# Second mixer: TensorE in written order with longer assumed latencies, zero-padded keys and factors, the last up-projection begun early

## The chip, the cores and the metric

The kernel runs on one core of a Trainium2 chip. The metric is the device time of one execution, in microseconds (us). An execution is also recorded by the hardware profiler: the rows of its trace are quoted below. PE is TensorE (matrix products), DVE VectorE, ACT ScalarE, POOL GpSimd, SP the engine that issues most of the DMAs.

## What is computed

256 tokens of width 1024 go through two layers (feed-forward, a mixer, feed-forward: a gated delta rule in the first, windowed attention in the second), a norm, and then a second block. Its mixer, which the change is about, is the sum of two gated branches over one input projection:

```python
proj = h @ w_in[i]
attn = windowed_gqa(q, k, v, sink[i])              # 8 query heads, 2 key heads of 64
rw = rwkv7_time_mix(zr, ...)                       # 8 heads of 64, scanned in both directions
gates = jax.nn.sigmoid(proj[..., O_GATE:].reshape(bsz, s, N_BRANCH, D_MODEL))
merged = gates[..., 0, :] * (attn @ w_up_attn[i]) + gates[..., 1, :] * (rw @ w_up_rwkv[i])
x = x + merged @ w_out[i]
```

`rwkv7_time_mix` makes a decay and a rate for each direction from low-rank factors (`w2`, `a2`, rank 64), normalises the keys, and runs this recurrence over the 256 tokens, forward and backward:

```python
sa = jnp.einsum('dbhij,dbhj->dbhi', state, a_t)
state = state * w_t[..., None, :] + sa[..., :, None] * b_t[..., None, :] + v_t[..., :, None] * k_t[..., None, :]
y = jnp.einsum('dbhij,dbhj->dbhi', state, r_t)
```

followed by a group norm, a bonus term and a gate.

## The kernel before

Weights are read as 128 x 1024 float32 tiles (`raw`), split by ACT and DVE into a high and a low half (`wh`, `wl`, L177 and L178), and each product of two split operands is three matmuls. In the second mixer these dense projections have 256 moving columns (`hT` against `wh`, `wl`).

The recurrence is computed in chunks of 64 tokens. The 512 channels make four channel tiles t = 0 to 3 of two heads each; `rw_chain(t)` is one such tile from its projections to its output: factors and decays (L1042 to L1130, tiles `lw`, `ta`, `cen`, `kd`, `BK`, `AR`), products of the factors (AR,BK), a triangular inverse (forward substitution on DVE, L430 to L443, then small products iY,Lc; iT,iX; iX,iT; iY,M on PE), then a scan of four steps over the chunks in both directions (R, UV, S; products UV,M; R,X; UV,bkt; S,AR), the group norm (L1240 to L1251), and the transposes and the gate into `sT[t]`. A step of the scan goes from PE to ACT (copy R, L1207), PE (R,X), DVE and ACT (copies UV, L1217 and L1218), PE (UV,bkt), DVE (state S, L1229) and PE again (S,AR). `gqa_chain` is the attention: a score product for each of 16 pairs of token half and head (kT,gt), a row maximum and exponential, transposes, products with v (v,sTl).

`weave` (L314) writes the five chains and a stream of projections into one program: each chain yields its PE time and the latency until its next step can run, the chain waits that latency times `slack`, and meanwhile projections are emitted. So the order in the program is a plan. In the kernel before, the order on each engine is then set anew by the scheduler of the tile framework, instruction by instruction, with a priority for the chains.

The stream holds the input projections (`p_rkv`, `p_q`, `p_kv`), the gates (`p_gate`) and the up-projections (`p_up`). The up-projection of the recurrent branch, which needs all four `sT[t]`, stands behind all chains, with the output projection `w_out`. Float32 matmuls are two records each in the trace, those on split operands and transposes one.

Of the kernel before, what the change touches and what calls it, by code (L numbers as in the profile page):

```python
# [9 lines left out]
F32 = mybir.dt.float32  # L10
# [5 lines left out]
P = 128  # L16
# [102 lines left out]
def _program(ctx, tc, a, out, stages):  # L119
# [302 lines left out]
    def tri_inverse(tl, Lc, off, nu, sign, unit, X, ydst=None):  # L422
# [551 lines left out]
    def mixer2_body(tl, hT, rstd, sums, finish_norm):  # L974
# [67 lines left out]
        def rw_chain(t):  # L1042
# [5 lines left out]
            w2a2, w0 = tl([256], "w2a2"), tl([256], "w0")  # L1048
            nc.sync.dma_start(w2a2, a["w2a2"][t])
# [4 lines left out]
            for m in range(2):  # L1054
                mm(ps[:, m * 256:(m + 1) * 256], wa[0:64, m * P:(m + 1) * P], w2a2[0:64])
# [5 lines left out]
            while state["k"][t] is None:  # L1061
                yield 0, 0.5
            k_ = state["k"][t]
# [21 lines left out]
            pbon = bank()  # L1085
            for d in range(2):
                ps = bank()
                mm(ps[:, 0:256], w2a2[64:128, d * P:(d + 1) * P], wa[64:128, :])
# [42 lines left out]
                yield 0.1, 2.0  # L1131
# [110 lines left out]
            for g in range(4):  # L1242
                junk = tl([64], "junk64")
                nc.scalar.activation(junk, py[:, g * 64:(g + 1) * 64], AF.Square, bias=nmean[:, g:g + 1],
                                     accum_out=var[:, g:g + 1])
# [12 lines left out]
            yield 0, 3.5  # L1258
# [32 lines left out]
        def gqa_chain():  # L1291
# [9 lines left out]
            kT, vs, qT = tl([256], "kT"), [], []  # L1301
            for m in range(2):
# [22 lines left out]
                ra, rb_, rc, rd = (tl([10, 8], f"rot{j}") for j in range(4))  # L1325
# [6 lines left out]
                yield 0, 6.0  # L1332
# [8 lines left out]
                nc.scalar.copy(kT[:, m * P:(m + 1) * P], ps[:, 0:P])  # L1341
# [4 lines left out]
            def scores(m, t, e):  # L1346
                hd, r = e * 4 + t, slice(e * 64, e * 64 + 64)
# [3 lines left out]
                ps = bank()  # L1351
                mm(ps[:, 0:256], qT[m][r, t * P:(t + 1) * P], kT[r, :])
                sm, mx = tl([256], "sTh", 4), tl([1], "mx", 2)
                nc.vector.tensor_tensor_reduce(out=sm, in0=ps[:, 0:256], in1=C(f"near{m}"), scale=1.0, scalar=-3e38,
                                               op0=ALU.add, op1=ALU.max, accum_out=mx)
                nc.vector.tensor_scalar(nm[:, hd:hd + 1], mx, -0.125, nsk[:, hd:hd + 1], ALU.mult, ALU.min)
                nc.scalar.activation(sm, sm, AF.Exp, scale=0.125, bias=nm[:, hd:hd + 1], accum_out=den[:, hd:hd + 1])
                return m, hd, e, sm
# [27 lines left out]
            todo = [(m, t, e) for m in range(2) for t in range(4) for e in range(2)]  # L1386
# [18 lines left out]
        def block_steps(src, blocks, ps):  # L1405
            for i, ap in enumerate(blocks):
                w = weights(ap)
                for q in range(4):
                    k = 4 * i + q
                    for h in range(2):  # L1410
                        for j, (l, r) in enumerate(((0, 0), (0, 1), (1, 0))):
                            mm(ps[:, h * 256:(h + 1) * 256], src[k][l][:, h * P:(h + 1) * P], w[r][:, q * 256:(q + 1) * 256],
                               k == 0 and h == 0 and j == 0, k == len(src) - 1 and j == 2, skip_group_check=True)
# [16 lines left out]

        def p_up(br, nb, pool=psA):
            ps = bank(pool)
            src = sTa if br == 0 else [sT[t] for t in range(NT)]
            yield from block_steps(src, [a["w_up_rwkv" if br else "w_up_attn"][nb]], ps)
# [30 lines left out]

        def stream():
# [8 lines left out]
        weave([rw_chain(t) for t in range(NT)] + [gqa_chain()], stream(), share=0.25, ahead=150, slack=0.95)  # L1475
# [220 lines left out]
```

## Time and profile before

| what | value |
| --- | --- |
| three timed runs, median | 1610.34 us (1604.14 to 1625.45) |
| the profiled execution's own time | 1610.71 us |
| its span in the trace | 1608.9 us |
| granted TensorE clock, mean over the span | 0.971 of full speed |
| PE busy | 1573.1 us, 98% of the span, 10608 records |
| DVE, ACT busy | 1097.5 us (68%), 919.4 us (57%) |

Busy times add up what an engine's records cover; on PE the ends of matmuls are modelled, so a high share does not mean that each matmul takes its shortest time. The interval from one start to the next is the better measure of a matmul's cost, and is used below.

### The profile page before, as it was taken

The page shows a single profiled execution, that of the slowest core. Times are in us where ns is not written, and L with a number is a line of the kernel's source. Part 1 is how long each engine was busy: PE and PEld are TensorE (multiplying, and loading weights), DVE is VectorE, ACT ScalarE, POOL GpSimd, SP SyncE. Part 2 cuts the span into 40 slices and gives each one's busy share as a digit, 9 for nine tenths or more (in the row PEclk, how much of TensorE's full clock was granted, in tenths as well). Part 3 has the DMA queues.
Part 4 walks back from the last instruction along what each step waited for, and adds up shares of the span by engine and source line. Part 5 has one row for each costly group of instructions (what it writes and reads, how often), then busy time and mean ns, then how long its engine had stood idle before and what let it go on. Part 6 is the DMA issues. An engine that isn't in the chain of part 4 may idle for free.

```text
span 1608.9 us, 28081 instructions
## 1 busy us (share of the span) xinstructions
PE 1573.1 (98%) x10608; PEld 1331.6 (83%) x10608; DVE 1097.5 (68%) x2691; ACT 919.4 (57%) x1998; POOL 36.6 (2%) x47
## 2 busy tenths in 40 slices
PE   7999998999999999999999999999999999999998
PEld 6888887997888888888888888888777788778887
DVE  6666779677766767666767766777756455776665
ACT  7555576666655555555546555575554444665553
POOL 0000010010000000000100000000000000000000
PEclk9999999999999999999999999998979679999999
DMA  7666523344766646665325766543211123565551
GB/s 230 208 197 196 172 61 107 100 150 133 236 195 197 192 135 212 197 198 161 118 90 161 212 196 199 165 143 112 70 31 32 36 83 119 177 223 194 195 185 55
DMA packets 71128, 244.18 MB, mean 152 GB/s; under 512 B 8400, under 2 KB 12240, under 8 KB 70992
## 3 DMA queue, kind: packets, MB, share of 16 engines
q1 hardware_dynamic: 70992, 242.39, 48.6%
q8 instruction: 83, 1.36, 0.3%
q14 instruction: 53, 0.43, 0.1%
HBM read 241.31 MB, written 1.05 MB: 151 GB/s over the span
## 4 chain that ended last, share of the span: by engine, by line
PE 76%; DVE 10%; DMA 8%; ACT 3%; issue 2%; POOL 1%; SPq 0%; ACTq 0%; DVEq 0%; POOLq 0%
PE bank L189 17%; PE bank L197 17%; PE bank L182 10%; PE bank L184 10%; PE bank L183 10%; PE bank L190 9%; DMA raw<-in_ffn_w_dram 5%; DVE wl L178 5%; ACT wh L177 2%; DMA raw<-in_w_ff_dram 1%; DVE cacc L596 1%; PE bank L248 1%; POOL rn L200 0%; DVE gs L194 0%; PE bank L1363 0%
## 5 line engine op out<-in xcount | busy, mean ns | idle before, releaser
L178 DVE TENSOR_TENSOR wl<-raw,wh 128x512 fp32r<-128x512 f32 (+1 forms) x714 | 574.8, 827 | 218.7 <-ACT wh L177 212.7
L177 ACT CAST wh<-raw 128x512 fp32r<-128x512 f32 (+1 forms) x714 | 497.4, 731 | 298.5 <-DMA raw<-in_ffn_w_dram 170.3
L189 PE MATMUL bank<-hT,wh 128*128 128x512 f32 x1664 | 587.6, 396 | 3.6 <-DVE hT L255 3.5
L190 PE MATMUL bank<-hT,wl 128*128 128x256 f32 x1664 | 463.3, 279 | 0.2 <-DVE wl L178 0.2
L189 PEld LDWEIGHTS bank<-hT,wh 128*128 128x128 f32 x1664 | 312.7, 188 | 77.6 <-DVE hT L255 5.7
L190 PEld LDWEIGHTS bank<-hT,wl 128*128 128x128 f32 x1664 | 313.5, 188 | 5.0 <-DVE wl L178 0.7
L182 PE MATMUL bank<-wh,aT 128*128 128x512 f32 x584 | 232.2, 398 | 3.1 <-ACT aT L216 2.8
L184 PE MATMUL bank<-wh,aT 128*128 128x512 f32 x584 | 229.1, 395 | 1.0 <-DVE aT L217 1.0
L183 PE MATMUL bank<-wl,aT 128*128 128x512 f32 x584 | 228.4, 391 | 0.0
L182 PEld LDWEIGHTS bank<-wh,aT 128*128 128x128 f32 x584 | 109.6, 188 | 29.0 <-ACT aT L216 5.4
L184 PEld LDWEIGHTS bank<-wh,aT 128*128 128x128 f32 x584 | 109.5, 188 | 28.9 <-DVE aT L217 3.6
L183 PEld LDWEIGHTS bank<-wl,aT 128*128 128x128 f32 x584 | 109.8, 188 | 19.7
L182 PE MATMUL bank<-hT,wh 128*128 128x256 f32 x384 | 114.3, 298 | 1.7 <-ACT wh L177 1.7
L184 PE MATMUL bank<-hT,wl 128*128 128x256 f32 x384 | 112.5, 294 | 0.6 <-DVE wl L178 0.6
L183 PE MATMUL bank<-hT,wh 128*128 128x256 f32 x384 | 112.7, 294 | 0.0
L402 ACT ACTIVATE gs<-gs 128x256 f32<-128x256 f32 x88 | 36.8, 418 | 85.9 <-DVE gs L401 85.9
L194 DVE TENSOR_TENSOR av<-av,bank 128x256 f32<-128x256 f32 x120 | 50.0, 418 | 43.9 <-ACT av L193 43.2
L182 PEld LDWEIGHTS bank<-hT,wh 128*128 128x128 f32 x384 | 75.6, 197 | 4.3 <-ACT wh L177 1.9
L184 PEld LDWEIGHTS bank<-hT,wl 128*128 128x128 f32 x384 | 75.4, 197 | 3.5 <-issue 2.1
L183 PEld LDWEIGHTS bank<-hT,wh 128*128 128x128 f32 x384 | 75.6, 197 | 2.2 <-issue 1.6
L197 PE MATMUL bank<-wh,hT 128*128 128x256 f32 x256 | 60.8, 322 | 0.1
L216 ACT CAST aT<-av 128x256 fp32r<-128x256 f32 x120 | 48.6, 406 | 21.2 <-DVE av L1519 12.3
(412 smaller groups left out, 2044.9 us busy)
## 6 DMA issues: line engine op xcount, KB each, us to landing
raw<-in_ffn_w_dram SPq DMA_DIRECT2D x264, 512.0 KB, 4.1
raw<-in_w_ff_dram SPq DMA_DIRECT2D x64, 512.0 KB, 4.2
raw<-in_a_w_qkv_dram SPq DMA_DIRECT2D x24, 512.0 KB, 3.7
raw<-in_w_gate_dram SPq DMA_DIRECT2D x16, 512.0 KB, 3.5
raw<-in_w_rwkv_dram SPq DMA_DIRECT2D x14, 512.0 KB, 3.6
raw<-in_b_w_qk_dram SPq DMA_DIRECT2D x10, 512.0 KB, 4.3
raw<-in_a_w_z_dram SPq DMA_DIRECT2D x8, 512.0 KB, 3.6
raw<-in_a_w_out_dram SPq DMA_DIRECT2D x8, 512.0 KB, 3.5
```

What stands on the lines that cost most here:

```text
L177: nc.scalar.copy(hi[:, c], raw[:, c])
L178: nc.vector.tensor_tensor(lo[:, c], raw[:, c], hi.bitcast(F32)[:, c], ALU.subtract)
L182: nc.tensor.matmul(o, l[0], r[0], start=start, stop=False, **kw)
L183: nc.tensor.matmul(o, l[0], r[1], start=False, stop=False, **kw)
L184: nc.tensor.matmul(o, l[1], r[0], start=False, stop=stop, **kw)
L189: nc.tensor.matmul(o, l[0], both, start=start, stop=False, skip_group_check=True)
L190: nc.tensor.matmul(o[:, 0:256], l[1], both[:, 0:256], start=False, stop=stop, skip_group_check=True)
L194: nc.vector.tensor_tensor(t, t, o[:, 0:256], ALU.add)
L197: nc.tensor.matmul(o, lhsT, rhs, start=start, stop=stop, **kw)
L216: nc.scalar.copy(hi, src)
L248: nc.tensor.transpose(ps[:, q * 256 + h * P:q * 256 + (h + 1) * P], x[h][n][:, c * P:(c + 1) * P], ident)
L402: nc.scalar.activation(gs, gs, AF.Silu)
```

## The change

- The second mixer's `weave` runs with the scheduler's reordering switched off for PE alone: PE gets its instructions in the order in which they are written. The other engines are scheduled as before.
- `slack` goes from 0.95 to 1.3, and some yields have longer latencies: 5.0 and 4.0 at the start of chain 0, 7.0 before the bonus products, 11.0 for 6.0 in the attention's prelude, 5.0 for 3.5 before the chain's last transposes.
- The factors of both directions are computed first, the bonus products (kd,rks) come later, with their own bank allocated later.
- The low-rank factors are held in two tiles padded with zeros to 128 rows (`w2z`, `a2z`), so these products have 128 rows; two DMAs for one in each chain.
- The keys are held as two copies padded with zeros (`kT`, [2, 256]): the scores of two heads are one product of 128 rows and 512 columns, 8 in all for 16; the attention goes on in pairs of heads.
- The recurrent branch's up-projection is begun for three of its four column blocks with channel tiles 0 to 2 (`p_begin`), while the last chain runs; `p_up` adds tile 3.
- Some small tiles share buffers with others, and `irow` has two buffers for three (in the first layer's mixer too).

```diff
-                row = tl([nu, 16], "irow", 3)[:, :, 0:k]
+                row = tl([nu, 16], "irow", 2)[:, :, 0:k]
...
+        w2z, a2z = tl([256], "w2z"), tl([256], "a2z")
+        nc.gpsimd.memset(w2z[64:128], 0.0)
+        nc.gpsimd.memset(a2z[0:64], 0.0)
...
-            w2a2, w0 = tl([256], "w2a2"), tl([256], "w0")
-            nc.sync.dma_start(w2a2, a["w2a2"][t])
+            if t == 0:
+                yield 0, 5.0
+            w0 = tl([256], "w0")
+            nc.sync.dma_start(w2z[0:64], a["w2a2"][t][0:64])
+            nc.sync.dma_start(a2z[64:128], a["w2a2"][t][64:128])
...
-                mm(ps[:, m * 256:(m + 1) * 256], wa[0:64, m * P:(m + 1) * P], w2a2[0:64])
+                mm(ps[:, m * 256:(m + 1) * 256], wa[:, m * P:(m + 1) * P], w2z)
...
-                mm(ps[:, 0:256], w2a2[64:128, d * P:(d + 1) * P], wa[64:128, :])
+                mm(ps[:, 0:256], a2z[:, d * P:(d + 1) * P], wa)
...
-                yield 1.3, 2.0
-                while state["r"][t] is None:
-                    yield 0, 0.5
-                r_ = state["r"][t]
+                facs.append((ta, Em, cen, off))
+                yield 0.9, 0
+            while state["r"][t] is None:
+                yield 0, 0.5
+            r_ = state["r"][t]
+            kds = []
+            for d, (ta, Em, cen, off) in enumerate(facs):
...
+                kds.append(kd)
+            yield 0, 7.0
+            pbon = bank()
+            for d, kd in enumerate(kds):
                 for m in range(2):
                     mm(pbon[:, 2 * m:2 * m + 2], kd[:, m * P:(m + 1) * P], rks[:, d * 4 + t], d == 0 and m == 0, d == 1,
...
-            yield 0, 3.5
+            yield 0, 5.0
...
-            kT, vs, qT = tl([256], "kT"), [], []
+            kT, vs, qT = tl([2, 256], "kT"), [], []
+            for e in range(2):
+                nc.gpsimd.memset(kT[64 - e * 64:128 - e * 64, e], 0.0)
...
-                yield 0, 6.0
+                yield 0, 11.0
...
-                mm(ps[:, 0:256], qT[m][r, t * P:(t + 1) * P], kT[r, :])
+                mm(ps, qT[m][:, t * P:(t + 1) * P], flat(kT))
...
-                if q2:
-                    values(*q2.pop(0))
-                if q1:
-                    q2.append(turn(*q1.pop(0)))
-                if todo:
-                    q1.append(scores(*todo.pop(0)))
-                yield 0.9, 1.2
+                for args in q2:
+                    values(*args)
+                q2 = [turn(*args) for args in q1]
+                q1 = scores(*todo.pop(0)) if todo else []
+                yield 1.8, 3.6
...
+        def p_begin(nb):
+            ps, w = begun[nb] = bank(psA), weights(a["w_up_rwkv"][nb])
+            yield from block_steps(sT, [None], ps, w, range(NT - 1))
...
         def p_up(br, nb, pool=psA):
+            if (br, nb) in ((1, k) for k in begun):
+                ps, w = begun[nb]
+                yield from block_steps(sT, [None], ps, w, [NT - 1])
+            else:
...
+        tasks += [(lambda nb=nb: len(gts) == 8 and state["rw"][2] > 2 and (nb < 1 or state["rw"][3] > 1), lambda nb=nb: p_begin(nb))
+                  for nb in range(3)]
...
-        weave([rw_chain(t) for t in range(NT)] + [gqa_chain()], stream(), share=0.25, ahead=150, slack=0.95)
+        with tc.manual_schedule(engines={mybir.EngineType.PE}):
+            weave([rw_chain(t) for t in range(NT)] + [gqa_chain()], stream(), share=0.25, ahead=150, slack=1.3)
```

Three places show what that makes of PE's order. The numbers in the names count the program's tiles, so they differ between the two programs. The first place is the start of the third chain's inverse (products iY,Lc), with a step of another chain's scan (UV,M and S,AR). Before:

```order
L197 MATMUL bank_13925<-iY_13673,Lc_13598 32x32 x6
L197 MATMUL bank_13999<-UV_13995,M_12453 64x64
L197 MATMUL bank_13925<-iY_13673,Lc_13598 32x32
L197 MATMUL bank_13999<-UV_13996,M_12531 64x64
L197 MATMUL bank_13925<-iY_13673,Lc_13598 32x32
L197 MATMUL bank_13999<-UV_13995,M_12453 64x64
L197 MATMUL bank_13925<-iY_13673,Lc_13598 32x32
L197 MATMUL bank_13999<-UV_13996,M_12531 64x64
L197 MATMUL bank_13925<-iY_13673,Lc_13598 32x32
L197 MATMUL bank_13999<-S_13325,AR_12157 64x128
L197 MATMUL bank_13925<-iY_13673,Lc_13598 32x32
```

After, the same chain's inverse, with an up-projection of the attention branch (wh, wl against sTh, sTl) around it:

```order
L197 MATMUL bank_14112<-wh_14115,sTl_13907 128x256
L197 MATMUL bank_14145<-iY_13881,Lc_13806 32x32 x32
L197 MATMUL bank_14112<-wh_14115,sTh_13913 128x256
L197 MATMUL bank_14112<-wl_14116,sTh_13913 128x256
L197 MATMUL bank_14112<-wh_14115,sTl_13914 128x256
L197 MATMUL bank_14112<-wh_14115,sTh_13913 128x256
L197 MATMUL bank_14112<-wl_14116,sTh_13913 128x256
L197 MATMUL bank_14112<-wh_14115,sTl_13914 128x256
L197 MATMUL bank_13669<-UV_14040,M_12882 64x64
L197 MATMUL bank_13669<-UV_14041,M_12947 64x64
L197 MATMUL bank_13669<-UV_14040,M_12882 64x64
L197 MATMUL bank_13669<-UV_14041,M_12947 64x64
```

The inverse's 32 products now stand together, as do the scan's.

The second place is the fourth chain's last step of the scan. Before, with a gate projection (wh, wl against hT) between:

```order
L197 MATMUL bank_15234<-UV_15230,M_14298 64x64
L197 MATMUL bank_14919<-wh_14922,hT_11329 128x256
L197 MATMUL bank_15234<-UV_15231,M_14350 64x64
L197 MATMUL bank_14919<-wl_14923,hT_11329 128x256
L197 MATMUL bank_14919<-wh_14922,hT_11329 128x256 x2
L197 MATMUL bank_15234<-S_14989,AR_14100 64x128 x2
L197 MATMUL bank_14919<-wl_14923,hT_11329 128x256
L197 MATMUL bank_14987<-S_14989,AR_14100 64x128
L197 MATMUL bank_14919<-wh_14922,hT_11329 128x256
L197 MATMUL bank_14987<-S_14989,AR_14100 64x128
L197 MATMUL bank_15247<-R_15241,X641_11372 64x64
```

After:

```order
L197 MATMUL bank_15255<-UV_15251,M_14436 64x64
L197 MATMUL bank_15255<-UV_15252,M_14494 64x64
L197 MATMUL bank_15255<-UV_15251,M_14436 64x64
L197 MATMUL bank_15255<-UV_15252,M_14494 64x64
L197 MATMUL bank_15255<-S_15039,AR_14126 64x128 x2
L197 MATMUL bank_15037<-S_15039,AR_14126 64x128 x2
L197 MATMUL bank_15266<-R_15262,X641_11372 64x64 x4
L197 MATMUL bank_15037<-UV_15251,M_14436 64x64
```

No projection is left between the products of this step, and none between it and the step ahead of it.

The third place is the end of the fourth chain, where its normed output is transposed (`aTl`, `aTh` against the identity in `c_base`) and gated (`gl` with `g2`). Before, among the gate projections:

```order
L197 MATMUL bank_15025<-wh_15084,hT_11429 128x256
L1262 MATMUL bank_15295<-c_base_78,aTh_15286 128x128
L197 MATMUL bank_15025<-wh_15084,hT_11429 128x256
L197 MATMUL bank_15025<-wl_15085,hT_11429 128x256
L197 MATMUL bank_15025<-wh_15084,hT_11429 128x256
L197 MATMUL bank_15025<-wh_15084,hT_11432 128x256
L1262 MATMUL bank_15295<-c_base_78,aTh_15286 128x128
```

After, behind the begun up-projection (tiles of `sT` of the third chain, sTh_15069 and sTl_15070), and ahead of what needs this chain's own output (sTh_15375):

```order
L197 MATMUL bank_15339<-wh_15342,sTh_15069 128x256
L197 MATMUL bank_15339<-wl_15343,sTh_15069 128x256
L197 MATMUL bank_15339<-wh_15342,sTl_15070 128x256
L1278 MATMUL bank_15364<-c_base_78,aTl_15306 128x128 x2
L1278 MATMUL bank_15364<-c_base_78,aTh_15305 128x128 x2
L197 MATMUL bank_15365<-gl_12163,g2_15312 128x256
L197 MATMUL bank_15171<-wh_15174,sTh_15375 128x256
```

All gates have moved ahead of this place; between the transposes and the products that need their result one other matmul stands.

## Rows read from the trace of the kernel before

**Rows 1.** The page, parts 1 and 4: busy time, its share of the span, instructions of each engine; and the chain that ended last, share of the span by engine.

```profile
PE 1573.1 (98%) x10608; PEld 1331.6 (83%) x10608; DVE 1097.5 (68%) x2691; ACT 919.4 (57%) x1998; POOL 36.6 (2%) x47
...
PE 76%; DVE 10%; DMA 8%; ACT 3%; issue 2%; POOL 1%; SPq 0%; ACTq 0%; DVEq 0%; POOLq 0%
```

**Rows 2.** Busy time of each engine in a stretch, the whole region of the second mixer's chains. Columns: stretch in us, its length, then busy us and records of each engine, mean granted clock of TensorE (1 is full), DMA share, GB/s.

```profile
1055.57:1363.58 308.01, 305.04 (x3008) 247.49 (x3009) 193.03 (x724) 160.07 (x400) 0.62 (x2) 0.87 0.23 73
```

**Rows 3.** The largest of PE's waits in that region: line waited at, engine and line waited for; us in total, times, longest.

```profile
PE bank L1363 <- ACT sTh L1357: 1.2, 1, 1.2
```

**Rows 4.** The six stretches of that region in which the granted clock is at half; columns as in the second group. The first of them, and the sum of all.

```profile
1115.00:1125.20 10.20, 10.20 (x70) 7.83 (x70) 4.03 (x12) 4.20 (x10) 0.00 (x0) 0.50 0.30 103
...
sum 81.70, PE 81.70 PEld 61.39 DVE 30.17 ACT 30.67 POOL 0.62; mean PE 13.62 PEld 10.23 DVE 5.03 ACT 5.11 POOL 0.10
```

**Rows 5.** The same columns for a stretch ahead of a fall of the clock and for one of dense gate projections.

```profile
1176.40:1183.30 6.90, 6.90 (x93) 5.21 (x91) 2.91 (x9) 4.30 (x12) 0.00 (x0) 0.99 0.28 79
...
1340.40:1347.20 6.80, 6.80 (x58) 6.80 (x58) 3.81 (x17) 4.74 (x14) 0.00 (x0) 1.00 0.27 80
```

**Rows 6.** PE in order of time, third chain's inverse and a scan. Columns: start, time until the last of the group ends (us), engine, line, operation, out<-in, shape, records in the group.

```profile
1232.59 0.31 PE L197 MATMUL bank<-iY,Lc 32*32 32x32 f32 x12
1232.84 0.33 PE L197 MATMUL bank<-UV,M 64*64 64x64 f32 x2
1233.09 0.24 PE L197 MATMUL bank<-iY,Lc 32*32 32x32 f32 x2
1233.27 0.33 PE L197 MATMUL bank<-UV,M 64*64 64x64 f32 x2
...
1234.38 0.27 PE L197 MATMUL bank<-iY,Lc 32*32 32x32 f32 x2
```

**Rows 7.** PE in order of time, the fourth chain's last two steps of the scan, and the transposes behind its norm; columns as before.

```profile
1326.09 0.66 PE L197 MATMUL bank<-S,AR 128*64 128x128 f32 x8
1326.67 0.39 PE L197 MATMUL bank<-wh,hT 128*128 128x256 f32 x1
...
1327.11 0.45 PE L197 MATMUL bank<-R,X 64*64 64x64 f32 x8
...
1327.85 0.45 PE L197 MATMUL bank<-UV,M 64*64 64x64 f32 x8
1328.23 0.50 PE L197 MATMUL bank<-wh,hT 128*128 128x256 f32 x2
...
1331.64 0.45 PE L197 MATMUL bank<-R,X 64*64 64x64 f32 x8
...
1335.70 0.38 PE L197 MATMUL bank<-wl,hT 128*128 128x256 f32 x1
1336.02 0.43 PE L197 MATMUL bank<-S,AR 128*64 128x128 f32 x2
1336.38 0.39 PE L197 MATMUL bank<-wh,hT 128*128 128x256 f32 x1
...
1347.56 0.33 PE L1262 MATMUL bank<-c_base,aTh 128*128 128x128 f32 x1
```

**Rows 8.** PE in order of time, three places: products of the factors cut off from each other, the same in one block, and a score product; columns as before.

```profile
1079.07 0.71 PE L197 MATMUL bank<-AR,BK 64*128 64x128 f32 x4
1079.71 0.61 PE L197 MATMUL bank<-rks,kd 128*128 128x2 f32 x4
...
1131.64 1.16 PE L197 MATMUL bank<-AR,BK 64*128 64x128 f32 x16
1132.73 0.28 PE L197 MATMUL bank<-zero 128*128 128x256 bf16 x1
...
1178.35 0.70 PE L197 MATMUL bank<-kT,gt 64*128 64x256 f32 x2
1178.98 0.38 PE L197 MATMUL bank<-rks,kd 128*128 128x2 f32 x2
```

**Rows 9.** DVE in order of time, first and last instruction of the third chain's forward substitution.

```profile
1208.99 0.42 DVE L430 TENSOR_TENSOR iLm<-Lc,c_inv 128x256 f32<-128x256 f32 x1
...
1229.66 0.44 DVE L443 STREAM_TRANSPOSE iX<-iY 128x256 f32<-128x256 f32 x1
```

**Rows 10.** DVE's groups of instructions in the region. Columns: line, engine, operation, out<-in, shapes, count, busy us, mean ns of one, idle time before and what ended it.

```profile
L178 DVE TENSOR_TENSOR wl<-raw,wh 128x1024 fp32r<-128x1024 f32 x41 | 49.9, 1220 | 10.7 <-ACT wh L177 10.5
...
L1229 DVE TENSOR_TENSOR S<-bank,sf 64x128 f32<-64x128 f32 x24 | 6.9, 287 | 14.2 <-PE bank L197 13.9
...
L1217 DVE COPY UV<-bank 64x128 f32<-64x128 f32 x16 | 4.6, 288 | 21.3 <-PE bank L197 21.2
```

**Rows 11.** DVE and then ACT in order of time, the tail: norm (L1240 to L1251), gate and split (L1265 to L1275), gated sum (L1436), split for the output projection (L217).

```profile
1340.27 0.42 DVE L1240 TENSOR_REDUCE nmean<-bank 128x4 f32<-128x256 f32 x1 [0.26 <-PE bank L197]
...
1352.06 0.42 DVE L1275 TENSOR_TENSOR sTl<-aTh,sTh 128x256 fp32r<-128x256 f32 x1
...
1357.82 0.68 DVE L1436 SCALAR_TENSOR_TENSOR gt<-gt,bank 128x512 f32<-128x512 f32 x1
...
1361.91 0.76 DVE L217 TENSOR_TENSOR aT<-bank,aT 128x256 fp32r<-128x256 f32 x2
...
1346.81 1.29 ACT L1251 ACTIVATE aTh<-bank,nmean,var 128x64 f32<-128x64 f32 x4
...
1348.52 0.57 ACT L1265 ACTIVATE aTh<-bank,vec 128x256 f32<-128x256 f32 x1 [0.42 <-PE bank L1262]
```

More of the change, by code (lines that the diff above doesn't have):

```diff
@@ L1324, in gqa_chain @@
                 x1, x2 = hx(qk)[:, :, 0:8], hx(qk)[:, :, 8:16]
-                ra, rb_, rc, rd = (tl([10, 8], f"rot{j}") for j in range(4))
+                ra, rb_, rc, rd = (tl([256], "sTl", 4)[:, 0:80].rearrange("p (h s) -> p h s", s=8) for j in range(4))
                 nc.vector.tensor_tensor(ra, x1, cos, ALU.mult)
@@ L1340, in gqa_chain @@
                 nc.tensor.transpose(ps[:, 0:P], qk[:, 512:640], ident)
-                nc.scalar.copy(kT[:, m * P:(m + 1) * P], ps[:, 0:P])
+                for e in range(2):
+                    nc.scalar.copy(kT[e * 64:e * 64 + 64, e, m * P:(m + 1) * P], ps[e * 64:e * 64 + 64, 0:P])
                 yield 0.5, 0.5
@@ L1344, in gqa_chain, with scores @@
             acc = {}
-            def scores(m, t, e):
-                hd, r = e * 4 + t, slice(e * 64, e * 64 + 64)
+            def scores(m, t):
                 if m not in acc:
@@ L1350, in scores @@
                 den, nm = acc[m]
-                ps = bank()
-                mm(ps[:, 0:256], qT[m][r, t * P:(t + 1) * P], kT[r, :])
[L1353 to L1358, printed above, removed]
+                ps, both = bank(), []
+                mm(ps, qT[m][:, t * P:(t + 1) * P], flat(kT))
+                for e in range(2):
+                    hd = e * 4 + t
+                    sm, mx = tl([256], "sTh", 4), tl([1], "mx", 2)
+                    nc.vector.tensor_tensor_reduce(out=sm, in0=ps[:, e * 256:(e + 1) * 256], in1=C(f"near{m}"), scale=1.0,
+                                                   scalar=-3e38, op0=ALU.add, op1=ALU.max, accum_out=mx)
+                    nc.vector.tensor_scalar(nm[:, hd:hd + 1], mx, -0.125, nsk[:, hd:hd + 1], ALU.mult, ALU.min)
+                    nc.scalar.activation(sm, sm, AF.Exp, scale=0.125, bias=nm[:, hd:hd + 1], accum_out=den[:, hd:hd + 1])
+                    both.append((m, hd, e, sm))
+                return both
             def turn(m, hd, e, pr):
@@ L1402, in gqa_chain, with block_steps @@
             state["gqa"] = True
-        def block_steps(src, blocks, ps):
+        def block_steps(src, blocks, ps, ws=None, only=range(8)):
             for i, ap in enumerate(blocks):
-                w = weights(ap)
+                w = weights(ap) if ws is None else ws
                 for q in range(4):
                     k = 4 * i + q
+                    if k not in only:
+                        continue
                     for h in range(2):
@@ L1412, in block_steps @@
                             mm(ps[:, h * 256:(h + 1) * 256], src[k][l][:, h * P:(h + 1) * P], w[r][:, q * 256:(q + 1) * 256],
-                               k == 0 and h == 0 and j == 0, k == len(src) - 1 and j == 2, skip_group_check=True)
+                               k == 0 and h == 0 and j == 0, k == 4 * len(blocks) - 1 and j == 2, skip_group_check=True)
                     yield 0.64, 0
@@ L1429, in p_gate @@
             gts[br, nb] = g
+        begun = {}
+        def p_begin(nb):
+            ps, w = begun[nb] = bank(psA), weights(a["w_up_rwkv"][nb])
+            yield from block_steps(sT, [None], ps, w, range(NT - 1))
         def p_up(br, nb, pool=psA):
-            ps = bank(pool)
-            src = sTa if br == 0 else [sT[t] for t in range(NT)]
-            yield from block_steps(src, [a["w_up_rwkv" if br else "w_up_attn"][nb]], ps)
+            if (br, nb) in ((1, k) for k in begun):
+                ps, w = begun[nb]
+                yield from block_steps(sT, [None], ps, w, [NT - 1])
+            else:
+                ps = bank(pool)
+                yield from block_steps(sT if br else sTa, [a["w_up_rwkv" if br else "w_up_attn"][nb]], ps)
             g = gts[br, nb]
```

10 lines of the change are left out of this document (6 added, 4 removed).

## The prediction

> **What bounds the kernel now.** I read the page first, then one table of stretches, PE's waits, and the order in time. The page has PE busy 98% of the span and 76% of the chain that ended last, with the granted clock below full mainly in one region [rows 1]. That region is the second mixer's chains: from its first small matmul (the diagonal transposed, 1055.57 us) to the first 512-column matmul of the last projection (1363.58), 308.0 us, with PE 305.0, DVE 193.0 and ACT 160.1 us busy and a mean clock of 0.87 [rows 2]. The edited code lies almost wholly in it. Busy here is not good use. PE waits for nobody: the longest single wait in these 308 us is 1.2 us [rows 3]. [...] Where the 16-row inverse (iY,Lc) and the scan (UV,M) alternate, two records of UV,M take 0.25 us, as long as twelve of iY,Lc in a row [rows 6]. So the region is bound by the order in which PE gets its work, and by the clock that goes with it, not by DVE, ACT or DMA.
>
> My account of the region, at the trace's own time: 308.0 = 40.9 lost to the clock + 3.0 idle (308.01 less 305.04) + 264 of issuing at full clock.
>
> **Fewer changes of kind.** Counted in the two orders between the same end points, taking the dense projections as one kind, PE has 496 runs of one kind of matmul before and 281 after, 215 fewer: UV,M 64 runs to 27, AR,BK 26 to 8, iX,iT 29 to 8, iY,Lc 26 to 4, v,sTl 24 to 8, scores 16 to 8. A run's price comes from the order in time. In the mixed stretch from 1232.59 to 1234.38 (1.79 us), eighteen records of iY,Lc at 21 ns (0.25 for twelve) and eight of UV,M at 48 ns (eight in 0.38 where they stand in one block) would be 0.76 us: 1.03 us for eight runs, 0.13 each [rows 6, 7]. Around the scan's last step, one projection between S,AR and R,X takes 0.32 instead of 0.12 and two S,AR 0.36 instead of 0.15 (eight in 0.58): 0.20 a run [rows 7]. AR,BK is dearer: four records 0.64 us when cut off, sixteen 1.09 us in a block that alternates the two halves of the rows [rows 8]; that is 0.16 against 0.07 each, 0.37 for a run of four. I take 0.14, near the first because most vanished runs are of its sort: 215 x 0.14 = 30 us. Bounds 0.10 (runs between kinds of like size) and 0.20: 22 and 43 us.
>
> **Padded keys and factors.** Sixteen score products on 64 rows and 256 columns (0.63 us from one start to the next [rows 8]) become eight on 128 rows and 512 columns. No row shows that shape in this type; two of the old ones (1.26) bound it above, one (0.63) below. I take 1.0, nearer the upper: 10.1 - 8.0 = 2 us, bounds 0 to 5. The decay and rate factors keep their count and columns, now on 128 rows: 0, bounds 1 us either way. Four more small DMAs on SP, four memsets on POOL (idle here) and two more 64-row ACT copies wait for nothing that PE waits for: 0. Weight transfers queue behind the extra DMAs, but DMA is at 0.23 [rows 2]. Fewer row buffers in the substitution (three to two, also in the first layer's mixer) only limit DVE against itself: 0, bounds 2 either way.
>
> So PE's own work becomes 264 - 30 - 2 = 232 us.
>
> **New waits.** In emission order a late input holds everything behind it, the projections too; before, they ran ahead. Three places lack cover.
> - Scan steps. One step runs 1327.11 to 1331.64, 4.5 us, with projections between [rows 7]. With none, the dependent part is about 3.7: R,X 0.4, DVE copy 0.3, ACT copy 0.3, UV,bkt 0.5, DVE on S 0.6, S,AR 0.4, ACT copy 0.3 and some 0.15 of hand-over for each of six (the DVE times [rows 10], the rest read off that step). PE's own work in such a step is about 2.4 us, so 1.3 is uncovered. The order after leaves six steps bare (the last three of the third and of the fourth chain): 8 us. Elsewhere the emission assumes (1.2 + 1.2 + 1.0) x 1.3 = 4.4 us, more than 3.7.
> - The forward substitution. DVE has it from 1208.99 to 1230.10 in the third chain, 21 us with other DVE work between [rows 9]. The emission now assumes 14 x 1.3 = 18.2 us (13.3 before), and only some 16 to 18 us of PE work stand there in the third and fourth chain: 0 to 6 us each, I take 5 together.
> - The tail. Before, gate projections, 58 of them in 6.80 us, ran up to the transposes at 1347.56 and on, and hid the norm [rows 5, 7]. They now come earlier; 36 matmuls of the begun up-projection (0.12 each, 4.3 us) stand there. The norm takes 1340.27 to 1348.10, less a 1.2 us weight split inside it [rows 10], with hand-overs some 6.5, so 2.2 wait. Then, from the transposes to the split factor, 1348.52 to 1352.48, of which about 3.0 is work of ACT and DVE, against three small PE runs of 0.4: 2.6. Then the last gated sum, its transposes and their split (0.68, as much for the sum, 0.8, and hand-overs: 4.9) less 18 projections already queued (2.2): 2.7. Together 7.5 [rows 11].
> Sum 20 us; bounds 8 (only the tail) and 45 (every substitution 6 late, twelve steps bare).
>
> **The clock.** The falls came while PE was hardly idle, in stretches with many small records: ahead of one, from 1176.4 to 1183.3, PE issued 93 of them and its weight loads fill 5.21 of 6.90 us, against all 6.80 in a dense stretch at full clock [rows 5]. In the new order blocks are compact and dense projections stand between, except in the bare steps of the third and fourth chain. I take one fall at each, as long as the first in the trace (10.2 us) [rows 4], 20 us in all at half: 10 us. Bounds 0 and the present 40.9.
> [...]
>
> **Sum.** 232 + 20 + 10 = 262 against 308, -46. The profiled execution is 1610.7 us (span 1608.9 and 1.8 around it), within 0.4 of the median 1610.34, so no correction: **1565 us**. A change of 2%, 32 us, is about what a measurement of this kernel can tell from none. Its own range, from the bounds of run price and waits, is 1545 to 1578.
>
> **Rivals.**
> - The clock keeps its share. 81.7 of 308 us are at half; if waits and small blocks keep that 27%, the region is (232 + 20) / (1 - 0.133) = 291 us: -17, **1593**. [...] Chance 0.14.
> - The helpers queue. DVE's 193 and ACT's 160 us of work, unchanged in count, must fit in some 250 us: 77% and 64% instead of 63% and 52%. The hand-overs on which PE stands (16 UV copies and 24 S on DVE alone [rows 10]; with the masks, row maxima and ACT's copies about 140) then come late; each 0.25 us later is 35 us: **1599**. Against it: on DVE they already wait for PE, UV 21.2 us and S 13.9 [rows 10]. Chance 0.11.
> - No cover missing and full clock: waits 8, clock 0, 240 us: -68, **1542**. For it: assumed latencies are above the measured ones in most places. Chance 0.17.
> - Slower: the substitution stops PE. DVE serves weight splits (41 of 1.22 us [rows 10]) between its small steps; if the blocks behind all four substitutions (18 to 22 us each) come half a substitution early, that is 40 us, with twelve bare steps (16) and the tail (7.5) 62 us of waits, and with the clock at its present share (232 + 62) / 0.867 = 339: +31, **1641**. It decides from 35 us of waits with that share, or 76 at full clock. Against it: a standing PE frees DVE, which then finishes sooner. Chance 0.07 for over 2% slower.
> - The change does nothing to the order: the orders above exclude it; what stays is that emission and chip agree less than I think, which the second and fourth hold.
>
> **How the numbers follow.** Forecast 0.51, of which 0.49 is faster by over 2%; with the third rival and the best of the first 0.67. Within 2%: the forecast's slow edge and most of the first two rivals, 0.25. Slower: the fourth and the worst of the second, 0.08. The range must leave out at most 0.2: from 1538 (just past the third rival) to 1602 (past the second).
>
> **What would show it.** Right: the region shortens to some 250 to 270 us; UV,M and iY,Lc records come in whole blocks; idle time before PE rises from 3 to some 20 us, most of it in the third and fourth chain's scans and the tail; half-clock time falls from 82 to some 20 us. Wrong: half-clock time stays above 60 us; single waits of many us before the inverse blocks; or PE's busy time in the region above 260 us, by which a run would cost less than 0.1 us.

## The result, and the profile after

The kernel after takes 1565.87 us in the median of 4 runs (1563.88 to 1568.78); the kernel before, timed beside it, 1611.26 us. The ratio is 0.9709, with a 95% interval of 0.964 to 0.9778: faster by 2.9%. 1565 was forecast.

The profiled execution has a span of 1567.0 us. The page, parts 1 and 4, beside [rows 1]:

```profile
PE 1510.5 (96%) x10592; PEld 1298.8 (83%) x10592; DVE 1101.2 (70%) x2691; ACT 918.8 (59%) x2000; POOL 36.9 (2%) x51
...
PE 82%; DVE 9%; DMA 4%; ACT 3%; issue 1%; POOL 1%; SPq 0%; ACTq 0%; DVEq 0%; POOLq 0%
```

PE's share fell while the kernel got faster: it now stands at times, and gets through its work faster in between. The region of the second mixer, between the same two matmuls as in [rows 2], columns as there:

```profile
1063.62:1320.39 256.77, 236.56 (x3004) 209.82 (x3003) 192.41 (x721) 159.88 (x400) 0.62 (x2) 0.96 0.28 85
```

It shortened from 308.0 to 256.8 us, by 51.2. It starts 8.05 us later (1055.57 before), and the rest of the kernel behind it takes 1.29 us more (246.6 for 245.3): -51.24 + 8.05 + 1.29 = -41.9, the difference of the spans. The stretches at half clock, for [rows 4]:

```profile
1142.10:1145.50 3.40, 3.40 (x30) 2.14 (x32) 2.52 (x10) 0.67 (x4) 0.00 (x0) 0.50 0.79 223
1189.90:1193.30 3.40, 3.40 (x146) 3.34 (x147) 2.70 (x6) 1.15 (x5) 0.00 (x0) 0.50 0.04 6
1234.30:1237.70 3.40, 3.00 (x133) 2.96 (x134) 3.40 (x12) 1.62 (x8) 0.00 (x0) 0.50 0.02 5
1275.20:1282.10 6.90, 6.55 (x158) 6.05 (x147) 1.58 (x7) 3.85 (x16) 0.00 (x0) 0.51 0.01 2
1316.20:1319.60 3.40, 3.21 (x16) 2.94 (x15) 2.55 (x5) 2.57 (x3) 0.00 (x0) 0.50 0.00 0
1039.70:1046.50 6.80, 6.53 (x19) 4.82 (x20) 2.94 (x4) 2.02 (x6) 0.00 (x0) 0.50 0.38 127
```

The first five lie in the region: 20.5 us for 81.7 before. The sixth lies ahead of it. PE's waits in the region, the longest first (line waited at, what it waited for; total, times, longest), for [rows 3]:

```profile
PE bank L197 <- DVE wl L178: 3.6, 1, 3.6
PE bank L197 <- DVE iY L442: 3.0, 2, 2.5
PE bank L197 <- DVE nmean L1257: 2.4, 1, 2.4
PE bank L197 <- ACT sTh L1290: 1.6, 1, 1.6
PE bank L197 <- DVE iT L451: 1.5, 1, 1.5
PE bank L1278 <- ACT aTh L1267: 1.2, 2, 1.0
PE bank L197 <- DVE UV L1233: 1.2, 3, 0.4
```

And PE in order of time around six waits, with a block of scores and one of the scan (the brackets give the idle time ahead), for [rows 6 to 8]:

```profile
1039.90 0.80 PE L182 MATMUL bank<-wh,aT 128*128 128x512 f32 x1 [2.29 <-ACT aT L216]
...
1141.41 0.39 PE L197 MATMUL bank<-wl,hT 128*128 128x256 f32 x1 [3.62 <-DVE wl L178]
...
1179.79 1.13 PE L197 MATMUL bank<-kT,gt 128*128 128x512 f32 x2 [0.24 <-ACT sTl L1387]
1180.35 0.68 PE L182 MATMUL bank<-hT,wh 128*128 128x256 f32 x1
1180.87 0.28 PE L183 MATMUL bank<-hT,wh 128*128 128x256 f32 x1
...
1182.79 0.45 PE L197 MATMUL bank<-UV,M 64*64 64x64 f32 x8
1183.17 0.66 PE L197 MATMUL bank<-S,AR 128*64 128x128 f32 x8
...
1189.89 1.08 PE L197 MATMUL bank<-iT,iX 32*32 32x32 f32 x64 [1.54 <-DVE iT L451]
...
1234.70 1.08 PE L197 MATMUL bank<-iT,iX 32*32 32x32 f32 x64 [2.42 <-DVE nmean L1257]
...
1273.52 0.74 PE L197 MATMUL bank<-iY,Lc 32*32 32x32 f32 x64 [2.54 <-DVE iY L442]
...
1315.40 0.38 PE L197 MATMUL bank<-wh,sTh 128*128 128x256 f32 x1 [1.63 <-ACT sTh L1290]
```

Put side by side with the list of half-clock stretches, each of these six falls comes within 2 us of the end of a wait of 1.5 us or more; before, in the region, the clock fell with PE busy in all of the 81.7 us at half [rows 4]. Blocks are whole: 64 records of iY,Lc in 0.67 us (to 1274.19), eight of UV,M in 0.38.

The account of the region for every kernel that ran, from its profiled execution. Idle is the region's length less PE's busy time; half is the sum of the stretches at half clock; issuing is what is left, length - idle - half / 2. The half is an estimate from the granted clock of 0.50 in these stretches (dense products of 256 columns follow each other there in 0.21 us for 0.12: before, 1123.54 to 1124.82 and 1340.50 to 1342.66). Where PE stood inside a stretch at half clock, that takes the standing off issuing one and a half times; the column "issuing, busy half" takes off idle time and half of what PE was busy at half clock instead. Runs of one kind are counted in the order, as in the prediction. Clock is the mean granted clock of the whole kernel, the median of its timed runs (for before, of the 55 fast runs timed beside the experiments).

| kernel | median us | clock | region | idle | half | issuing | issuing, busy half | runs of one kind |
| --- | --- | --- | --- | --- | --- | --- | --- | --- |
| before | 1611 to 1614 | 0.971 | 308.0 | 3.0 | 81.9 | 264.1 | 264.1 | 496 |
| e1 (sched): after, scheduler orders PE | 1602.5 | 0.9765 | 302.0 | 3.1 | 68.3 | 264.7 | 264.7 | 549 |
| e2 (order_only): before, written order | 1616.8 | 0.9675 | 311.3 | 37.9 | 92.2 | 227.3 | 234.2 | 363 |
| e3 (order_slack): e2 with slack 1.3 | 1603.7 | 0.977 | 295.1 | 36.1 | 51.2 | 233.5 | 236.7 | 339 |
| e5 (bonus): e3, factors first, bonus later | 1608.8 | 0.971 | 296.6 | 37.1 | 64.9 | 227.0 | 233.4 | 337 |
| e9 (bonus_yields): e5, longer latencies | 1590.0 | 0.975 | 281.1 | 22.9 | 54.6 | 230.9 | 233.1 | 313 |
| e6 (timing): e9, heads in pairs | 1580.0 | 0.977 | 272.5 | 24.3 | 44.4 | 226.0 | 228.5 | 280 |
| e7 (nopad): e6, up-projection begun | 1578.6 | 0.978 | 277.0 | 19.1 | 64.9 | 225.4 | 226.6 | 281 |
| e8 (nobegin): e6, padded | 1571.0 | 0.984 | 258.7 | 23.9 | 20.5 | 224.5 | 226.7 | 280 |
| e12 (keys_only): e7, keys padded | 1573.2 | 0.983 | 261.0 | 19.2 | 23.9 | 229.8 | 230.9 | 281 |
| after | 1565.9 | 0.987 | 256.8 | 20.2 | 20.5 | 226.3 | 226.8 | 281 |
| e4 (slack095): after, slack 0.95 | 1575.6 | 0.9815 | 264.7 | 25.7 | 30.7 | 223.6 | 229.0 | 324 |
| e10 (tuned): after, longer inverse | 1571.3 | 0.9835 | 258.6 | 22.1 | 23.9 | 224.6 | 227.0 | 273 |
| e11 (slack15): after, slack 1.5 | 1584.3 | 0.9785 | 270.6 | 28.3 | 34.1 | 225.2 | 226.4 | 264 |

Each row's account is of one execution, and executions of one kernel differ in the clock: the kernel before was timed between 1594 us (clock 0.981) and 1628 us (0.960). e1's profiled execution is the slowest of its ten runs and e7's the slowest of its four; those of e4, e11 and e12 are the fastest of theirs. So the column half is compared here together with the clock of all runs. (1 - clock) x time, an estimate of what the low clock costs, is some 47 us before and 20 after: 26 of the 45 us between the medians.

### The profile page after: what moved, and what is told of

Its sections match the earlier page's. It is cut to its first block, busy times and chain, and to the rows that moved or that the text cites. A ratio compares the mean times of both kernels' runs of the same rounds, so it can differ in the third digit from the quotient of the medians.

```text
span 1567.0 us, 28074 instructions
## 1 busy us (share of the span) xinstructions
PE 1510.5 (96%) x10592; PEld 1298.8 (83%) x10592; DVE 1101.2 (70%) x2691; ACT 918.8 (59%) x2000; POOL 36.9 (2%) x51
## 4 chain that ended last, share of the span: by engine, by line
PE 82%; DVE 9%; DMA 4%; ACT 3%; issue 1%; POOL 1%; SPq 0%; ACTq 0%; DVEq 0%; POOLq 0%
PE bank L189 22%; PE bank L197 12%; PE bank L182 12%; PE bank L184 12%; PE bank L183 11%; PE bank L190 11%; DVE wl L178 3%; DMA raw<-in_w_ff_dram 1%; ACT wh L177 1%; PE bank L248 1%; DMA raw<-in_ffn_w_dram 1%; DVE cacc L596 1%; DMA raw<-in_w_rwkv_dram 0%; DVE irow L438 0%; PE bank L851 0%
## 5 line engine op out<-in xcount | busy, mean ns | idle before, releaser
L182 PE MATMUL bank<-wh,aT 128*128 128x512 f32 x584 | 233.4, 400 | 5.5 <-ACT aT L216 5.2
L197 PE MATMUL bank<-wh,hT 128*128 128x256 f32 x256 | 57.6, 306 | 2.1 <-DVE hT L255 2.1
```

The costliest lines, as they stand in the source:

```text
L182: nc.tensor.matmul(o, l[0], r[0], start=start, stop=False, **kw)
L197: nc.tensor.matmul(o, lhsT, rhs, start=start, stop=stop, **kw)
```

## The experiments

**The order alone, and everything but the order.**

```diff
# e1, from the kernel after
-        with tc.manual_schedule(engines={mybir.EngineType.PE}):
-            weave([rw_chain(t) for t in range(NT)] + [gqa_chain()], stream(), share=0.25, ahead=150, slack=1.3)
+        weave([rw_chain(t) for t in range(NT)] + [gqa_chain()], stream(), share=0.25, ahead=150, slack=1.3)
# e2, from the kernel before; e3 the same with slack=1.3
-        weave([rw_chain(t) for t in range(NT)] + [gqa_chain()], stream(), share=0.25, ahead=150, slack=0.95)
+        with tc.manual_schedule(engines={mybir.EngineType.PE}):
+            weave([rw_chain(t) for t in range(NT)] + [gqa_chain()], stream(), share=0.25, ahead=150, slack=0.95)
```

> The kernel after, but with the scheduler ordering PE again (slack 1.3 and all else stay). Theory (the gain is PE's order: fewer changes of kind and with them more clock): its PE order has 549 runs of one kind in the region against 281 after and 496 before, so the gain goes: 1600 to 1625 us, half-clock time in the region above 60 us, idle time of PE there under 6 us. Rival (padding, longer latencies and the begun up-projection bring most of it): under 1585 us.

e1: 1602.5 us, ratio 0.9956 (0.9919 to 0.9992). All the other edits together are worth 0.4% when the scheduler orders PE: issuing is 264.7 us for 264.1 and half-clock time is 68.3. The theory held. The padding is in e1 too, so in the scheduler's order it did not go with as little half-clock time as in the kernel after (20.5).

> The kernel before, with nothing changed but that PE keeps the written order in the second mixer (slack 0.95, old latencies). 363 runs for 496: 133 x 0.14 = 19 us less issuing. Theory (order pays, but the old latencies are too short, so PE stands): waits of 30 to 45 us in the region, most at the inverses' first products, and 1580 to 1600 us. Rival (latencies do not matter, the order alone does it): waits near the 20 us of the kernel after and 1565 to 1575 us. A third: waits eat the whole gain, above 1610 us.

e2: 1616.8 us, ratio 1.002 (0.9997 to 1.0043), no gain. Issuing fell by 36.8 us, or by 29.9 when standing at half clock is not taken off it; PE stood for 37.9 us, 13.9 of them with the clock down, and the clock was down for 92.2 us, some 10 more than before. The third case came out. The region, the sum of its stretches at half clock, and the longest waits:

```profile
1058.86:1370.12 311.26, 273.33 (x3016) 231.67 (x3015) 196.48 (x723) 160.22 (x397) 0.62 (x2) 0.85 0.23 72
...
sum 92.10, PE 78.16 PEld 65.87 DVE 38.27 ACT 34.22 POOL 0.00; mean PE 8.68 PEld 7.32 DVE 4.25 ACT 3.80 POOL 0.00
```

```profile
PE bank L197 <- DVE kd L1127: 10.9, 4, 4.3
PE bank L1262 <- ACT aTh L1251: 5.6, 1, 5.6
PE bank L197 <- DVE iYc L440: 5.4, 1, 5.4
PE bank L197 <- ACT wa L1022: 3.2, 1, 3.2
```

The bonus products (kd), which the program writes straight behind the DVE work that makes kd, cost most; then the norm, the inverse and the low-rank input.

> The kernel before, with PE in written order and slack 1.3, and none of the other edits. 339 runs: 157 x 0.14 = 22 us less issuing. Theory: waits near 25 us, 1572 to 1585 us: most of the gain of the kernel after, the rest (5 to 15 us) belonging to the other edits (pairs of scores, factors first, extra latencies). Rival (the other edits carry the gain): above 1595 us.

e3: 1603.7 us, ratio 0.9943 (0.991 to 0.9975). The rival held: slack alone gives 13 us over e2, and 38 are left to the other edits. The waits are nearly as long as in e2, since slack lengthens only latencies that are written:

```profile
PE bank L197 <- DVE kd L1127: 8.4, 5, 4.0
PE bank L197 <- DVE rsq L210: 6.4, 1, 6.4
PE bank L1262 <- ACT aTh L1251: 5.3, 1, 5.3
PE bank L1335 <- DVE qk L1331: 4.2, 1, 4.2
PE bank L197 <- ACT wa L1022: 3.3, 1, 3.3
```

**Where the other edits' gain lies.** e5 puts the loops of both directions apart and a `yield 0, 7.0` ahead of the bonus products, as the change's diff has it, into e3. e9 adds the change's longer yields (5.0 and 4.0 at chain 0, 11.0 and 5.0). e6 adds the attention in pairs of heads.

> The kernel before with PE in written order and slack 1.3 (as the run order_slack, 1603.7 us), and of the other edits one: both directions' factors first, the bonus products (kd,rks) later behind a latency of 7.0. Theory (a step written ahead of its data costs its wait and a fall of the clock): the 8.4 us that PE stood for kd in order_slack go, with 5 to 10 us of half clock: 1586 to 1596 us, and the waits for wa, for qk at the attention's transposes and for the norm stay. Rival (the wait moves to the next step): 1600 to 1606 us.

e5: 1608.8 us, ratio 0.9974 (0.9936 to 1.0011). The rival's mechanism held, 2.8 us above its range. The wait for kd is gone, and its time is found at the next steps:

```profile
PE bank L1342 <- DVE qk L1338: 8.9, 2, 5.4
PE bank L197 <- DVE iY L442: 8.2, 1, 8.2
PE bank L1269 <- ACT aTh L1258: 5.3, 1, 5.3
PE bank L197 <- ACT wa L1022: 3.6, 1, 3.6
```

Idle time is 37.1 us against 36.1. Mending one step of a chain that PE reaches too early lets PE reach the next one too early.

> The run bonus (1608.8 us) with the longer latencies as well: 5.0 and 4.0 at the start of chain 0, 11.0 for 6.0 before the attention's transposes, 5.0 for 3.5 before a chain's last transposes. It differs from the run timing (1580.0) only in that the attention goes head by head with 1.2 of latency instead of in pairs with 3.6. Theory (the waits are where a step stands ahead of its data, and a step's own latency mends it): the waits for wa and qk go (12 us), idle time in the region falls from 37 to some 25 us, 1585 to 1595 us. Rival (the pairs of heads bring it): above 1600 us.

e9: 1590.0 us, ratio 0.9888 (0.9856 to 0.992). Now idle time falls to 22.9 us; the waits for wa and qk are not among the larger ones any more. The theory held.

> The kernel after without the padded keys and factors (two score products on 64 rows, each with a bank of its own, for one on 128) and without the up-projection begun early: order, slack and latencies alone. Theory (order and latencies are the gain): 1566 to 1578 us, idle time in the region 20 to 30 us. Rival (padding or the begun projection carries the 37 us between order_slack and the kernel after): above 1585 us.

e6: 1580.0 us, ratio 0.9771 (0.971 to 0.9832), 2 us above the theory's range: order, slack, latencies and pairs make 32 us of the change's 45. What it has beyond e9, the pairs and the shared small buffers together, adds 10 us with idle time about the same: half-clock time falls by 10 us and issuing by 5.

**Padding and the begun up-projection.** e7 is the kernel after without padding, with two score products in banks of their own; e12 pads the keys alone; e8 leaves the begun projection out.

```diff
# e7, scores
-                mm(ps, qT[m][:, t * P:(t + 1) * P], flat(kT))
+                for e in range(2):
+                    r = slice(e * 64, e * 64 + 64)
+                    mm(pss[e][:, 0:256], qT[m][r, t * P:(t + 1) * P], kT[r, :])
# e7 and e12, factors
-                mm(ps[:, m * 256:(m + 1) * 256], wa[:, m * P:(m + 1) * P], w2z)
+                mm(ps[:, m * 256:(m + 1) * 256], wa[0:64, m * P:(m + 1) * P], w2a2[0:64])
# e8
-                  for nb in range(3)]
+                  for nb in range(0)]
```

> The kernel after without the padded keys and factors (score products on 64 rows, two banks). By the sum of the prediction padding is worth 2 us (0 to 5): 1566 to 1571 us. Rival (two products on different halves of the rows run side by side, so that padding loses): 1562 to 1565 us.

e7: 1578.6 us (1573.7 to 1585.2), ratio 0.9763 (0.9698 to 0.9828). Neither case: padding is worth some 13 us of the medians, more than its bound of 5, and not by the time of its own matmuls. e6 and e8 differ by the same edit, without the begun projection: 9 us. Issuing is 225.4 us against 226.3, idle time 19.1 against 20.2. The clock makes the difference: over the four runs it was 0.972 to 0.981 in e7 (0.976 to 0.981 in e6), and 0.984 to 0.988 in the kernel after (0.981 to 0.985 in e8). The stretches at half in e7's profiled execution, longest of them and sum:

```profile
1199.70:1223.60 23.90, 23.90 (x227) 20.42 (x223) 9.78 (x35) 12.64 (x42) 0.31 (x1) 0.50 0.15 45
...
sum 64.90, PE 62.64 PEld 53.62 DVE 29.82 ACT 33.52 POOL 0.31; mean PE 10.44 PEld 8.94 DVE 4.97 ACT 5.59 POOL 0.05
```

64.9 us at half for 20.5. The pair of half-row products itself takes no longer than one: both are done in 0.63 us where they are issued next to each other (from one start to the next):

```profile
1147.62 0.70 PE L197 MATMUL bank<-kT,gt 64*128 64x256 f32 x4
1148.25 0.44 PE L1152 MATMUL bank<-c_base,p_v 128*128 128x128 f32 x2
```

The padded one takes 0.86 with the same product behind it, in the kernel after:

```profile
1149.40 1.02 PE L197 MATMUL bank<-kT,gt 128*128 128x512 f32 x2
1150.26 0.38 PE L1156 MATMUL bank<-c_base,p_v 128*128 128x128 f32 x2
```

The place shown above (1179.79 to 1180.35, 0.56) looks shorter, but is no measure of it: the dense product behind it starts early, and the one after that follows 0.52 us later (1180.87), where dense products else follow each other in 0.12. So as plain time padding costs 0.23 us a pair against a pair side by side, as the rival had it; what goes with it is the higher clock (0.987 for 0.978 in the median of the runs).

> The kernel after with the padded keys but the factors unpadded (w2a2 on 64 rows, as before). The run nopad lost 12.7 us with idle time and full-clock issuing unchanged: its half-clock time in the region rose from 20.5 to 64.9 us. Theory (64-row products let the clock fall, and the score products are the ones that stand where it fell, from 1152 to 1224 us): half-clock time 20 to 35 us, 1564 to 1571 us. Rival (the factors' products, which stand near the same places, count as much): half-clock time 40 to 55 us, 1572 to 1577 us.

e12: 1573.2 us (1568.1 to 1579.9), ratio 0.9766 (0.9707 to 0.9825). The half-clock time of 23.9 us lies in the theory's range, but it is that of the fastest of the four runs; the median lies in the rival's. Over the four runs the clock was 0.980 to 0.987, between e7 and the kernel after. So the padded keys and the padded factors both seem to count for the clock, and with four runs each the shares of the 13 us are not settled.

> The kernel after without the up-projection begun early: the same matmuls come after the last chain. By the prediction 36 matmuls (4.3 us) then no longer stand in the tail's norm: 3 to 8 us more with the clock that falls there, 1569 to 1574 us. Rival (the norm's wait is hidden otherwise): 1564 to 1567 us.

e8: 1571.0 us (1570.2 to 1572.2), ratio 0.9716 (0.9645 to 0.9786): 5.1 us more than the kernel after, as expected. The wait stands where the prediction put it; the transposes behind the last norm, to be read against the 0.99 us of the kernel after:

```profile
1309.67 1.07 PE L1278 MATMUL bank<-c_base,aTh 128*128 128x128 f32 x2 [5.27 <-ACT aTh L1267]
```

Idle time rises by 3.7 us. Between e6 and e7, without padding, the same edit gives 1.5 us, within their spread.

**The latencies, shorter and longer.**

> The kernel after with slack 0.95 for 1.3. 324 runs for 281: 43 x 0.14 = 6 us more issuing. Theory: the inverses' blocks come 5 us early each (13.3 for 18.2 us assumed), scans some 1.1 us a step: waits of 30 to 45 us in the region for 20, and 1577 to 1592 us. Rival (the waits stay as they are, since a standing PE lets DVE finish sooner): 1568 to 1575 us.

e4: 1575.6 us, ratio 0.9765 (0.9721 to 0.9809), between the two cases: idle time 25.7 us, of which 11.7 for iY in two waits, the longer 10.3.

```diff
# e10
-        yield 0, 14.0
+        yield 0, 14.0 if sign > 0 else 16.5
-        yield 0.15 * nu, 1.6
+        yield 0.15 * nu, 1.6 if sign > 0 else 3.2
```

> The kernel after with longer latencies at the two places where PE still stands for the inverse: 16.5 for 14.0 for the second mixer's forward substitution, 3.2 for 1.6 behind iY,Lc. Theory: the waits for iY and iT (some 6 us of the region's 20) go, with one to three falls of the clock (1.7 us each): 1557 to 1563 us. Rival (the whole chain comes later and the tail gets the same time): 1565 to 1570 us.

e10: 1571.3 us, ratio 0.9788 (0.9725 to 0.9851), slower than the kernel after by 5: the rival's case, 1.3 us above its range. The waits for iT went, but one for iY of 3.7 us took their place, the one for wl grew to 4.7, and idle time is 22.1 us.

> The kernel after with slack 1.5 for 1.3; 264 runs for 281. Theory: at 1.3 most latencies are covered, so more of it only shifts the chains back, and projections run out ahead of the tail: 1564 to 1575 us. Rival (the remaining waits are all short latencies): 1555 to 1562 us.

e11: 1584.3 us, ratio 0.9875 (0.9801 to 0.9948): worse than both cases. Idle time is 28.3 us and half-clock time 34.1, with 6.5 us for iY and 3.7 for iT. That later chains leave less dense work between their own steps is a reading, not shown. None of the variants beats the kernel after.

## Why the prediction was right, point by point

**The account.** The prediction had 232 us of issuing, 20 of waits and 10 for the clock, 262 in all; measured are 226.3, 20.2 and, as half of 20.5, 10.2, 256.8. The region's terms hold within 6 us. No run shows that a matmul at half clock takes twice as long, as the 40.9 us lost to the clock before (half of 81.7) assume. At a granted clock of 0.50 dense products of 256 columns followed each other in 0.21 us for 0.12 (before, places above), those of 512 columns in 0.43 for 0.23 (after, 1042.21 to 1043.91 and 1046.97 to 1047.90), and 64 records of iX,iT took 1.02 us, 62 of them 0.64 at full clock (after, 1190.73 and 1145.90). By these ratios the 40.9 would be some 29 to 37 us, and the 264 of issuing before 4 to 12 more. Of the region's 51.2 us the clock gave by this account 30.7 ((81.9 - 20.5) / 2), and issuing less the new waits 20.6 (37.8 - 17.2); 31 and 15 were forecast. That the total agrees within 1 us is luck, since 9.3 us were lost outside the region, where 0 was forecast.

**Fewer changes of kind.** The gain was put at 30 us and scores at 2; together they are 37.8. The mechanism is right: e1 has the scheduler's order and no gain in issuing, and e2 has the written order and most of it, 29.9 (issuing, busy half). The price was too simple: e1 has 53 runs more than the kernel before and the same issuing; from before to e2 a vanished run is worth 29.9 / 133 = 0.22 us; and among the kernel after, e4, e10 and e11, which differ in latencies alone, 324 runs take 229.0 us and 264 take 226.4, 0.04 a run. A price of 0.14 per run is not one to carry on.

**Scores.** One padded product takes 0.86 us to the next start (0.95 and 0.96 at two other places of the kernel after), a little less than the 1.0 assumed. So the plain gain over single products is 16 x 0.63 - 8 x 0.9 = 2.9 us for 2: right. The larger effect was not forecast at all: without padding the clock is down 44 us longer in the profiled execution of e7, half of which is 22; by the clocks of all runs, 0.978 and 0.987, it is some 14 us.

**Waits.** 20 us is right in sum and wrong in its places. Of the scan's bare steps, put at 8 us, at most 2.7 are found (UV 1.2, R 1.0, S 0.5); of the tail's 7.5, some 3.0 (sTh 1.6, aTh 1.2, gt 0.2); of the inverse's 5, 3.0 for iY. The place of the rest is DVE: 3.6 us for a weight split, and 2.4 and 1.5 for iT (the 2.4 are put down to nmean, which DVE did right behind iT). DVE in order of time before the longest of them:

```profile
1138.33 0.41 DVE L1137 TENSOR_TENSOR AR<-p_r,cen 128x256 f32<-128x256 f32 x1
1138.67 0.41 DVE L1138 TENSOR_TENSOR AR<-kn,cen 128x256 f32<-128x256 f32 x1
1139.00 0.41 DVE L1139 TENSOR_TENSOR kd<-kd,p_r 128x256 f32<-128x256 f32 x1
1139.34 0.41 DVE L451 TENSOR_TENSOR iT<-bank,c_inv 128x256 f32<-128x256 f32 x1
...
1140.15 1.21 DVE L178 TENSOR_TENSOR wl<-raw,wh 128x1024 fp32r<-128x1024 f32 x1
```

The products of both directions' factors now come as one burst of DVE work, and the split that PE needs stands behind it. That is the second rival's mechanism (helpers queue) at 7.5 us, not 35. The burst is read off the trace; no run spread it out again with all else equal.

**The clock.** 20 us at half were forecast and 20.5 came, but one fall at each bare stretch of the scans was the reasoning, and that step failed: five falls came at five waits, so the agreement is luck. What a wait of PE costs in clock was weighed too lightly: in the trace after the clock fell at each of the six waits of 1.5 us and more from 1039.90 us on, for 3.4 to 6.9 us. But such a wait has no fixed price. e8 has the waits for iT and for iY at the same places, and the clock stayed up in them and for 3 us and more behind them (its column is the third from the end):

```profile
1189.82 0.71 PE L197 MATMUL bank<-iT,iX 32*32 32x32 f32 x62 [1.54 <-DVE iT L451]
...
1272.34 0.74 PE L197 MATMUL bank<-iY,Lc 32*32 32x32 f32 x64 [2.53 <-DVE iY L442]
```

```profile
1188.30:1230.80 42.50, 38.12 (x641) 32.35 (x641) 34.17 (x151) 28.92 (x87) 0.62 (x2) 1.00 0.14 39
1269.80:1275.30 5.50, 2.79 (x209) 2.46 (x208) 3.69 (x14) 0.36 (x2) 0.00 (x0) 1.00 0.07 25
```

What brought the clock down before, with PE idle for 3.0 us of the region, stays open. In the written order the clock was down longer with half-row products: e7 has the new order, and still 64.9 us at half, for 20.5 in the kernel after. In the scheduler's order that is not shown: e1 has the padding, and 68.3 us at half. The first rival (the clock keeps its share) comes nearest in e7, with 64.9 of 277.0 us, and not here.

**Outside the region.** The prediction put the rest of the kernel at nothing. The first layer's mixer, whose order changed too, lost 1.6 us (the first matmul behind it on its split output stands at 1033.31 for 1031.76), and 6.5 went from there to the region: the last split of that output (aT) came late on ACT, behind a weight split that waited 1.51 us for its DMA, PE stood 2.29 us for it, and the clock fell for 6.8. The order on ACT and SP is the same there in both kernels, and before, ACT waits 1.57 us for the same DMA; but SP issues these five transfers from 1029.19 us on for 1024.93, 4.3 us later. The same wait of PE is found with 2.7 us in e1, where the scheduler orders PE, with 3.5 in e9 and 0.8 in e10; its cause is open. Neither loss is shown to be the change's: e2, e3, e5 and e9 leave the first layer's mixer as it was and reach the same matmul 0.7 to 3.0 us later than the profiled execution of the kernel before, and in every other kernel that ran the region starts 2.8 to 10.1 us later than in that execution.

## What to carry to other kernels

Written order on the engine that is the bound pays only together with latencies that match the trace at every step of a chain: alone it gained 30 us of issuing and gave back 35 in waits (e2), and mending a single step moved the wait to the next one (e5). Read which waits are left in the trace, mend them all, and stop there: latencies longer by 15% cost 18 us (e11). Compare idle time, half-clock time and issuing apart from each other, since an edit can act through one of them alone, and look at the clock of all timed runs, since one profiled execution can be the slowest or the fastest of its kernel. And measure a matmul's cost where the same work follows in both kernels: the start of the next one alone can deceive.

## What the hardware showed

- Two 64-row products on different halves of the rows, issued next to each other, took 0.63 us together (e7, 1147.62), as long as one alone before [rows 8] (0.70 to the end of the second; 0.97 at another place of e7, 1195.18); the zero-padded product of the same work took 0.86 with the same product behind it (the kernel after, 1149.40).
- In the written order the clock was down longer with half-row products: 64.9 us at half with them (e7) and 20.5 with zero-padded ones (the kernel after), at about the same idle time and issuing, and 0.972 to 0.981 of the clock against 0.984 to 0.988 over four runs each. The padded keys also have 512 columns for 256, so it is not shown that the rows alone do it; in the scheduler's order (e1) there were 68.3 us at half with the padded ones.
- In the profiled execution of the kernel after, each of the six waits of 1.5 us or more from 1039.90 us on had at least 3.4 us at half clock at or just behind its end, by the account's estimate 1.7 us and more beyond the wait; in e8 two of the same waits were followed by none.
